# Five half gates of a hybrid decoder layer move from plain tiles into groups with a seven-product scheme

## The chip, the cores and the metric

The kernel runs on one core of one Trainium2 chip. The metric is device time in microseconds (us). Five engines matter: PE (TensorE, matrix products and transposes), ACT (ScalarE), DVE (VectorE), POOL (GpSimd, nearly idle here) and SP (SyncE, which issues the weight loads). Each executes its own instructions in the order of the program and waits for the others by semaphores.

## What is computed

A decoder layer on 256 positions of 2048 channels in float32. One wide projection of the normed input feeds three token mixers (attention, gated linear attention, spatial gating) and three gates. The part that the change touches begins where the mixers have delivered their outputs:

```python
    proj = xn @ w_in
    ...
    qa, ka, va, qb, kb, vb, rb, lrb, uc, vc, ga, gb, gc = jnp.split(proj, splits, axis=-1)
    ...
    merged = (jax.nn.sigmoid(ga) * (y_a @ wa) + jax.nn.sigmoid(gb) * (y_b @ wb)
              + jax.nn.sigmoid(gc) * (y_c @ wc))
    h = x + merged @ w_o
    hn = rms_norm(h, n2)
    return h + jnp.square(jax.nn.relu(hn @ w1)) @ w2
```

`ga`, `gb`, `gc` are the three gates, each 2048 wide, and each needs a product of the whole normed input (2048 deep) with its own 2048 columns of `w_in`.

## The kernel before

**Precision.** Every float32 operand is split in two fp32r parts, high and low: ACT copies the high part (`whi`, `fhi`), DVE subtracts it from the operand and leaves the low part (`wlo`, `flo`). A product of two blocks is then three matmuls: high by high, high by low, low by high. Activations stand transposed in `xT`, `yT`, `mT`, `hT` and `fT`, split once; the weights are split as they stream in, so each megabyte of weights costs ACT and DVE a pass each.

**Plain groups.** `group_a` (L214 on) makes 512 output columns for both halves of the positions: for two k-tiles at a time it splits a weight piece of 128x1024 (L203, L204) and runs twelve matmuls of 128x512 (L221 to L223), six for each half of the positions. After every such piece `step()` may emit one queued job, such as a transpose. Before, the three gates and the three branch products were all made so, 512 columns at a time: a loop of four rounds over `n`, with three gates (sigmoid on ACT, L710) and three branch products (multiplied and added on DVE, L715 and L717) in each. In this stretch the order on the engines is the scheduler's.

**Fixed-order groups.** The output projection (`w_o`) and the feed-forward (`w_ff1`, `w_ff2`) run as `Group` objects of 1024 columns, with the order of all four busy engines written out (`manual_schedule`). A group of 2048 deep consists of eight pairs of k-tiles, taken as its order string says. A pair written `P` is a plain one: 24 matmuls. A pair written `S` uses the seven-product scheme for 2x2 blocks and takes 21: it comes in two pieces, A (9 matmuls) and B (12). For an S pair DVE first forms sums of weight blocks (`fsum`, L807 to L809), and these are split too. The other operand of an S pair are four sums of activation blocks (`sums`, made in `turn_into` on L683 to L689 from a transposed tile `half`, of which there are two buffers): four DVE operations on 128x128 blocks, an ACT copy of the high part (L688), a DVE subtraction for the low part (L689). `hT` and `fT` have three S pairs (3, 5, 6), the merged tile `mT` has two (6, 7).

**Order of work.** The loop over pieces `i` emits the split of piece `i + 2` (`ready`, `LEAD = 2`), then the matmuls of piece `i`. The split parts have three buffers. A group with S pairs ends by combining its eight accumulators on DVE (`seven` and four adds), and its results are transposed into the next activation tile while the next group runs: the transposes of one half (`turns`) stand after that group's first piece, those of the other half in the middle of its second piece.

**What sets the time of a turn.** In `turn_into` the block sums of a tile stand right behind its copies: ACT copies `half` from PSUM, copies the high part, then waits for DVE's four block sums, then copies their high part.

Of the kernel before, what the change touches and what calls it, by code (L numbers as in the profile page):

```python
# [11 lines left out]
F32 = mybir.dt.float32  # L12
# [6 lines left out]
P = 128  # L19
T = 256  # L20
# [43 lines left out]
def trunk(ctx: ExitStack, tc: tile.TileContext, x, rpe_table, norm1_g, w_in, q_norm_g, k_norm_g,  # L64
# [598 lines left out]
    def turn_into(dst, ks, srcs, gain=None, kinds=None, fn=AF.Copy):  # L663

        banks = []
        for s in srcs:
            banks.append(bank("tt"))
            transpose4(banks[-1], s)
        for k, ps in zip(ks, banks):
            if kinds is None:  # L670
                split_ps(dst[:, k:k + 2, :], v3(ps, 2))
                continue
            a = mpool.tile([P, 2, T], F32, tag="half", name="half", bufs=2)
            if gain is None:
# [54 lines left out]
    mg_ctx.__exit__(None, None, None)
    w_ctx.__exit__(None, None, None)  # L730
    ffp = ctx.enter_context(tc.tile_pool(name="ffp", bufs=1, reuse_waits="tile"))
    hT = acts.tile([P, KT, 2 * T], F32R, tag="act0", name="hT")

    sums = acts.tile([P, 8, 2, 4, P], F32R, tag="act1", name="sums")
    hS = {kp: sums[:, i] for i, kp in enumerate(SEVEN)}
    fS = {kp: sums[:, 4 + i] for i, kp in enumerate(SEVEN)}
    mS.update({kp: sums[:, 4 + i] for i, kp in enumerate(SEVEN_O)})
    hsq = gpool.tile([P, NT, 4], F32, name="hsq")
    r2 = gpool.tile([P, NT], F32, name="r2")
    hs = gpool.tile([P, NT], F32, name="hs")  # L740
# [259 lines left out]
```

## Time and profile before

| | us |
|---|---|
| median of 3 runs | 1455.39 |
| lowest, highest | 1454.23, 1455.61 |
| the profiled execution, its own time | 1454.36 |
| its span | 1452.6 |
| gates and branches, about | 303 to 649 |
| `w_o`, feed-forward, about | 649 to 1447 |

The span is what the profile covers; the execution's own time is 1.76 us longer. Times below are counted from the span's start. The granted clock of PE is given as a share of full speed: 1.00 is 2.4 GHz, 0.50 is 1.2 GHz. An engine's idle time counts only where the work that ends last waits in it.

### The profile page before, as it was taken

To read this page: it belongs to the slowest core of one execution; us is meant where nothing else is said; L and a number is where in the kernel's file an instruction comes from. 1 tells how busy PE (TensorE), PEld (TensorE's weight loads), DVE (VectorE), ACT (ScalarE), POOL (GpSimd) and SP (SyncE) were. 2 spreads that over 40 slices of the span, in tenths; PEclk is the share of its full clock that TensorE was granted. 3 is DMA by queue.
4 is the path that set the end of the run, shared out by engine and by line. 5 is a ranking of instruction groups with operands and counts; after the bars stand their busy time and mean duration, and the time that the engine had idled before them with its cause. 6 is when DMAs were issued, how large, how long until landed. Compare 5 with 4: busy or idle time off the path is not lost.

```text
span 1452.6 us, 16287 instructions
## 1 busy us (share of the span) xinstructions
PE 1422.9 (98%) x6452; PEld 1168.5 (80%) x6452; DVE 1072.9 (74%) x1160; ACT 766.5 (53%) x827; POOL 14.0 (1%) x37
## 2 busy tenths in 40 slices
PE   8999999999999999999998999999999999999998
PEld 6899887788888888877886878888788887888776
DVE  5655655454645546457898989999999999999898
ACT  7457444454444444445656654466644665546653
POOL 2000000000000000000000000000000000000000
PEclk9999999999999999999999999999999999999999
DMA  8555554545555555545555555666456555555553
GB/s 290 183 181 165 182 176 133 184 151 199 192 185 203 177 199 187 190 158 193 199 185 192 173 175 197 208 203 203 147 200 207 199 203 174 201 190 194 198 195 124
DMA packets 101948, 272.20 MB, mean 187 GB/s; under 512 B 4748, under 2 KB 11440, under 8 KB 101872
## 3 DMA queue, kind: packets, MB, share of 16 engines
q1 hardware_dynamic: 100944, 268.59, 55.0%
q0 software_dynamic: 928, 2.57, 0.5%
q8 instruction: 50, 0.82, 0.2%
q14 instruction: 26, 0.21, 0.0%
HBM read 268.26 MB, written 2.88 MB: 187 GB/s over the span
## 4 chain that ended last, share of the span: by engine, by line
PE 70%; DVE 18%; issue 6%; ACT 5%; DMA 0%; SPq 0%; DVEq 0%; ACTq 0%
PE c L768 22%; PE ga L221 14%; PE ga L223 14%; PE ga L222 14%; DVE flo L795 8%; PE P L768 4%; DVE fsum L807 3%; ACT fhi L794 3%; DVE fsum L808 2%; DVE fsum L809 2%; PE tt L235 1%; DVE fT L175 1%; PE pst L590 0%; ACT sums L688 0%; ACT half L675 0%
## 5 line engine op out<-in xcount | busy, mean ns | idle before, releaser
L204 DVE TENSOR_TENSOR wlo<-wraw,whi 128x1024 fp32r<-128x1024 f32 (+3 forms) x232 | 266.2, 1152 | 248.6 <-ACT whi L203 248.4
L203 ACT ACTIVATE whi<-wraw 128x1024 fp32r<-128x1024 f32 (+3 forms) x232 | 231.4, 1002 | 292.4 <-PE ga L223 284.9
L794 ACT ACTIVATE fhi<-fraw 128x2048 fp32r<-128x2048 f32 (+2 forms) x145 | 252.9, 1750 | 163.6 <-PE c L768 115.3
L795 DVE TENSOR_TENSOR flo<-fraw,fhi 128x2048 fp32r<-128x2048 f32 (+2 forms) x145 | 300.0, 2080 | 48.0 <-ACT fhi L794 48.0
L221 PE MATMUL ga<-whi,xT 128*128 128x512 f32 (+2 forms) x768 | 297.8, 388 | 0.0
L222 PE MATMUL ga<-wlo,xT 128*128 128x512 f32 (+2 forms) x768 | 293.4, 382 | 0.0
L223 PE MATMUL ga<-whi,xT 128*128 128x512 f32 (+2 forms) x768 | 293.1, 382 | 0.0
L768 PE MATMUL c<-fhi,hT 128*128 128x512 f32 x736 | 237.7, 390 | 0.0
L768 PE MATMUL c<-fhi,fT 128*128 128x512 f32 x736 | 237.1, 390 | 0.0
L221 PEld LDWEIGHTS ga<-whi,xT 128*128 128x128 f32 x768 | 144.6, 188 | 29.8 <-issue 3.9
L223 PEld LDWEIGHTS ga<-whi,xT 128*128 128x128 f32 x768 | 144.6, 188 | 26.9
L222 PEld LDWEIGHTS ga<-wlo,xT 128*128 128x128 f32 x768 | 144.7, 188 | 25.0
L768 PEld LDWEIGHTS c<-fhi,hT 128*128 128x128 f32 x736 | 138.2, 188 | 28.6
L768 PEld LDWEIGHTS c<-fhi,fT 128*128 128x128 f32 x736 | 138.2, 188 | 28.4
L794 ACT ACTIVATE fhi<-fsum 128x1024 fp32r<-128x1024 f32 x104 | 108.6, 1059 | 85.7 <-DVE fsum L807 41.0
L768 PE MATMUL c<-flo,fT 128*128 128x512 f32 x368 | 143.7, 391 | 3.3 <-DVE flo L795 3.3
L768 PE MATMUL c<-flo,hT 128*128 128x512 f32 x368 | 143.2, 389 | 0.0
L795 DVE TENSOR_TENSOR flo<-fsum,fhi 128x1024 fp32r<-128x1024 f32 x104 | 122.5, 1219 | 1.4 <-ACT fhi L794 1.4
L768 PE MATMUL P<-fhi,sums 128*128 128x512 f32 x312 | 106.0, 394 | 4.2 <-ACT fhi L794 4.0
L768 PEld LDWEIGHTS c<-flo,fT 128*128 128x128 f32 x368 | 69.1, 188 | 19.1 <-DVE flo L795 4.9
L768 PEld LDWEIGHTS c<-flo,hT 128*128 128x128 f32 x368 | 69.1, 188 | 14.1
L768 PEld LDWEIGHTS P<-fhi,sums 128*128 128x128 f32 x312 | 59.3, 190 | 18.4 <-ACT fhi L794 6.3
(260 smaller groups left out, 1427.1 us busy)
## 6 DMA issues: line engine op xcount, KB each, us to landing
fraw<-in_w_ff_dram SPq DMA_DIRECT2D x128, 1024.0 KB, 5.0
wraw<-in_w_in_dram SPq DMA_DIRECT2D x80, 1024.0 KB, 4.9
fraw<-in_w_o_dram SPq DMA_DIRECT2D x16, 1024.0 KB, 5.3
wraw<-in_w_br_b_dram SPq DMA_DIRECT2D x8, 1024.0 KB, 5.0
wraw<-in_w_in_dram SPq DMA_DIRECT2D x8, 692.0 KB, 4.1
wraw<-in_w_br_a_dram SPq DMA_DIRECT2D x4, 1024.0 KB, 4.9
wraw<-in_w_br_c_dram SPq DMA_DIRECT2D x4, 1024.0 KB, 5.4
wraw<-in_w_in_dram SPq DMA_DIRECT2D x6, 512.0 KB, 11.4
```

Of the source, the lines that this page charges most:

```text
L175: nc.vector.tensor_tensor(lo, ps, hi.bitcast(F32), ALU.subtract)
L203: nc.scalar.activation(hi[:, j:j + per, :w], src, AF.Copy)
L204: nc.vector.tensor_tensor(lo[:, j:j + per, :w], src, hi[:, j:j + per, :w].bitcast(F32), ALU.subtract)
L221: mm(ps[tt][:, :w], xh, hi[:, j, :w], start=(k == 0), stop=False)
L222: mm(ps[tt][:, :w], xh, lo[:, j, :w], start=False, stop=False)
L223: mm(ps[tt][:, :w], xl, hi[:, j, :w], start=False, stop=(k == nk - 1))
L768: mm(self.banks[role], a, w, start=(n == 0), stop=(n == self.total[role] - 1))
L794: nc.scalar.activation(hi[:, i:e], src[:, i - a:e - a], AF.Copy)
L795: nc.vector.tensor_tensor(lo[:, i:e], src[:, i - a:e - a], hi[:, i:e].bitcast(F32), ALU.subtract)
L807: nc.vector.tensor_tensor(ts[:, 0:2], raw[:, 1:3], raw[:, 0:1].to_broadcast([P, 2, GW]), ALU.add)
L808: nc.vector.tensor_add(ts[:, 2], ts[:, 0], raw[:, 2])
L809: nc.vector.tensor_add(ts[:, 3], ts[:, 2], raw[:, 3])
```

## The change

- The first half (1024 columns) of the first gate stays plain, in two `group_a` of 512 columns; the second of them now lies inside the written-out order. The other five half gates become groups of 1024 columns with the order `ORDER_G`, four S pairs (2, 3, 5, 6) and four P pairs. The branch products become groups of P pairs alone, 1024 columns wide, with two, four and two pairs.
- The S pairs of the gates need block sums of the normed input. `xs_turn` makes them for four pairs: four transposes of `h`, two scaling copies on ACT, then the block sums at once. The four calls stand behind the first four pieces of the second `group_a`.
- `w_o` has its S pairs at 2 and 3 instead of 6 and 7, in another order.
- `turn_into` no longer makes the block sums on the spot: they are emitted one piece later, behind the split that `ready` emits there (`run(i, "early")`). The squares for the second norm now stand behind the split of one piece more.
- From the first gate on there is one pool layout: the merged tile takes `yT`'s place, `hT` takes `xT`'s, `fT` takes the merged tile's; the block sums share two small pools; there are three `fu` buffers.

```diff
-ORDER_O = "P0 P1 P2 P3 P4 S6 S7 P5".split()
-SEVEN = [int(c[1]) for c in ORDER if c[0] == "S"]
-SEVEN_O = [int(c[1]) for c in ORDER_O if c[0] == "S"]
+ORDER_O = "P0 P1 S2 P6 S3 P4 P5 P7".split()
+ORDER_G = "P0 P1 S2 S3 P4 S5 S6 P7".split()
...
+    pg = [group_a(w_in[0], 0, KT, C_GATE, 512, xT)]
+    drain()
+    br_ctx.__exit__(None, None, None)
+    early_ctx.__exit__(None, None, None)
...
+    def kinds_of(pairs, tag, bufs, per):
+        out = {}
+        for i in range(0, len(pairs), per):
+            t = ffp.tile([P, per, 2, 4, P], F32R, tag=tag, name="kinds", bufs=bufs)
...
+        nc.scalar.activation(s[:, 0], b, AF.Copy)
+        nc.vector.tensor_tensor(s[:, 1], b, s[:, 0].bitcast(F32), ALU.subtract)
...
-            a = mpool.tile([P, 2, T], F32, tag="half", name="half", bufs=2)
+            a = ffp.tile([P, 2, T], F32, tag="half", name="half", bufs=2)
...
             if k // 2 in kinds:
-
-                b = a.rearrange("p j (t c) -> p (j t) c", c=P)
-                nc.vector.tensor_sub(b[:, 3], b[:, 1], b[:, 3])
-                nc.vector.tensor_sub(b[:, 1], b[:, 0], b[:, 1])
-                nc.vector.tensor_sub(b[:, 0], b[:, 3], b[:, 0])
-                nc.vector.tensor_add(b[:, 2], b[:, 2], b[:, 0])
-                s = kinds[k // 2]
-                nc.scalar.activation(s[:, 0], b, AF.Copy)
-                nc.vector.tensor_tensor(s[:, 1], b, s[:, 0].bitcast(F32), ALU.subtract)
...
+                rest.append(lambda a=a, s=kinds[k // 2]: block_sums(a, s))
+
+        def sums():
+            for f in rest:
+                f()
+        return sums if rest else None
...
-            pg = group_a(w_in[0], 0, KT, C_GATE + i * D + n * 512, 512, xT)
...
-            pp = group_a(wsrc[0], 0, nk, n * 512, 512, yT, k0=k0)
-            for tt in range(NT):
-                nc.vector.tensor_mul(gts[i][tt], pp[tt], gts[i][tt])
-                if i:
-                    nc.vector.tensor_add(gts[0][tt], gts[0][tt], gts[i][tt])
...
-            return [lambda: None, lambda: turns(hT, n, 1, src, V_N2, hS, AF.Copy),
-                    lambda: turns(hT, n, 0, src, V_N2, hS, AF.Copy), norm]
+            return [None, lambda: turns(made["hT"], n, 1, src, n2c, hS, AF.Copy),
+                    lambda: turns(made["hT"], n, 0, src, n2c, hS, AF.Copy), norm]
...
+            def sigmoid():
+                for tt in range(NT):
+                    v = u[:, 2 * tt:2 * tt + 2]
+                    nc.scalar.activation(v, v, AF.Sigmoid, scale=r[:, tt:tt + 1])
+            if (i, hf) == (2, 1):
+                mS.update(kinds_of(seven_of(ORDER_O), "xs", 1, 4))
+                m = gates[0, 0]
+                return [sigmoid, lambda: merged_turn(0, 0, m), lambda: merged_turn(0, 1, m)]
+            return [sigmoid]
...
+                    nc.vector.tensor_mul(v, g.banks[f"c{tt + 1}{2 - c}"], v)
+            if i:
+                m = gates[0, hf]
+                nc.vector.tensor_add(m, m, u)
+            if (i, hf) == (2, 1):
+                hS.update(kinds_of(seven_of(ORDER), "fu", 3, 2))
+                made["hT"] = acts.tile([P, KT, 2 * T], F32R, tag="act0", name="hT")
+                return [None, lambda: merged_turn(1, 1, m), lambda: merged_turn(1, 0, m)]
...
+    mT = yT
+    made = {}
+    xS = kinds_of(seven_of(ORDER_G), "xs", 1, 4)
...
+    for hf in range(2):
+        for i, (wsrc, k0, nk) in enumerate(((w_br_a, 0, 4), (w_br_b, 4, 8), (w_br_c, 12, 4))):
+            if (i, hf) != (0, 0):
+                groups.append(Group(w_in[0], 0, C_GATE + i * D + hf * W2, xT, xS, ORDER_G, *gate_in(i, hf)))
+            groups.append(Group(wsrc[0], 0, hf * W2, yT, {}, [f"P{j}" for j in range(nk // 2)], *branch_in(i, hf), k0))
...
+    def xs_turn(kp):
+        srcs = [h[:, tt, (2 * kp + j) * P:(2 * kp + j + 1) * P] for j in range(2) for tt in range(NT)]
+        turn_into(None, [2 * kp], [srcs], g1[0], xS)()
+
+    todo = {}
+
+    def run(i, when):
+        for fn in todo.pop((i, when), ()):
+            rest = fn and fn()
+            if rest:
+                todo.setdefault((i + 1, "early"), []).insert(0, rest)
+
+    fetched = []
     with tc.manual_schedule(engines=ORDERED):
+        u = gates[0, 0] = new_u()
+
+        def first_sigmoid(c):
+            for tt in range(NT):
+                nc.scalar.activation(u[:, 2 * tt + c], pg[c][tt], AF.Sigmoid, scale=r[:, tt:tt + 1])
+        first_sigmoid(0)
+        for kp in seven_of(ORDER_G):
+            later(lambda kp=kp: xs_turn(kp))
+        pg.append(group_a(w_in[0], 0, KT, C_GATE + 512, 512, xT))
+        w_ctx.__exit__(None, None, None)
+        hlp = ctx.enter_context(tc.tile_pool(name="hlp", bufs=1, side="right", reuse_waits="tile"))
         for i in range(LEAD):
             ready(i)
+        first_sigmoid(1)
...
-            since = i - done
-            if since == 1 and after:
-                after[0]()
-            multiply(piece, wts.pop(i), half=after[2] if since == 2 and after else None)
-            if since == 1 and after:
-                after[1]()
-            if since == 2 and len(after) > 3:
-                after[3]()
-            step()
+            run(i, "early")
+            multiply(piece, wts.pop(i), half=lambda: run(i, "half"))
+            run(i, "half")
+            run(i, "late")
             if ends:
-                after, done = g.last(g), i
+
+                for (d, when), fn in zip(((1, "early"), (1, "late"), (2, "half"), (3, "early")), g.last(g)):
+                    todo.setdefault((i + d, when), []).append(fn)
 
 
 # ---- launch: one core; inputs and outputs as the reference has them ----
```

ACT's instructions around the first gate's end, before (names: `whi` a weight piece's high part, `yT` the branch input, `ga` an accumulator of a gate, `gt` the gate, numbers tell tiles apart):

```order
L203 ACTIVATE whi<-wraw 128x1024 x2
L174 ACTIVATE yT<-ybt 128x2x256
L203 ACTIVATE whi<-wraw 128x1024 x3
L710 ACTIVATE gt_2587<-ga_2412,r 128x512
L710 ACTIVATE gt_2587<-ga_2413,r 128x512
L203 ACTIVATE whi<-wraw 128x1024 x8
```

The same place now (`half` is a transposed tile, `kinds` the block sums, `fu` the gate):

```order
L208 ACTIVATE whi<-wraw 128x1024 x2
L179 ACTIVATE yT<-ybt 128x2x256
L208 ACTIVATE whi<-wraw 128x1024
L1015 ACTIVATE fu<-ga_2412,r 128x512
L1015 ACTIVATE fu<-ga_2413,r 128x512
L208 ACTIVATE whi<-wraw 128x1024
L707 ACTIVATE half<-tt,g_150 128x256 x2
L692 ACTIVATE kinds<-half 128x512
L208 ACTIVATE whi<-wraw 128x1024
L707 ACTIVATE half<-tt,g_150 128x256 x2
L692 ACTIVATE kinds<-half 128x512
L208 ACTIVATE whi<-wraw 128x1024
```

Before, two or more splits of the next group stood ahead of the sigmoids; now the sigmoids stand ahead of the next group's first split, and two `half` copies and one `kinds` copy stand ahead of each of the four splits after it.

ACT in the first `w_ff2` group of a phase, from the first turn on, before:

```order
L688 ACTIVATE sums<-half 128x512
L675 ACTIVATE half<-tt 128x512
L174 ACTIVATE fT<-half 128x2x256
L794 ACTIVATE fhi<-fraw 128x1536
L675 ACTIVATE half<-tt 128x512
L174 ACTIVATE fT<-half 128x2x256
L675 ACTIVATE half<-tt 128x512
L174 ACTIVATE fT<-half 128x2x256
L688 ACTIVATE sums<-half 128x512
L794 ACTIVATE fhi<-fsum 128x1024 x2
L794 ACTIVATE fhi<-fraw 128x2048
```

The same place now:

```order
L772 ACTIVATE fhi<-fraw 128x1536
L692 ACTIVATE kinds<-half 128x512
L704 ACTIVATE half<-tt 128x512
L179 ACTIVATE fT<-half 128x2x256
L704 ACTIVATE half<-tt 128x512
L179 ACTIVATE fT<-half 128x2x256
L772 ACTIVATE fhi<-fsum 128x1024 x2
L692 ACTIVATE kinds<-half 128x512
L772 ACTIVATE fhi<-fraw 128x2048
```

Each copy of block sums moved behind a split: the first from ahead of the A piece (`fhi<-fraw` 128x1536) to behind it, the second from ahead of the B piece (`fhi<-fsum`) to between it and the next P piece (`fhi<-fraw` 128x2048).

## Rows read from the trace of the kernel before

**Rows 1.** The page, parts 1 and 4: busy engines, and the last chain by engine.

```profile
PE 1422.9 (98%) x6452; PEld 1168.5 (80%) x6452; DVE 1072.9 (74%) x1160; ACT 766.5 (53%) x827; POOL 14.0 (1%) x37
...
PE 70%; DVE 18%; issue 6%; ACT 5%; DMA 0%; SPq 0%; DVEq 0%; ACTq 0%
```

**Rows 2.** Stretches: span, busy PE, PEld, DVE, ACT, POOL, granted clock, DMA share, GB/s.

```profile
313.00:648.00 335.00, 335.00 (x1491) 277.35 (x1490) 173.03 (x164) 149.18 (x153) 0.00 (x0) 1.00 0.57 189
649.20:651.80 2.60, 0.19 (x1) 0.00 (x0) 2.56 (x5) 0.00 (x0) 0.00 (x0) 1.00 0.23 16
652.10:655.40 3.30, 3.30 (x9) 2.52 (x9) 2.99 (x2) 0.00 (x0) 0.00 (x0) 0.50 0.94 344
...
762.60:768.10 5.50, 0.92 (x3) 0.19 (x1) 2.29 (x5) 5.41 (x12) 0.00 (x0) 1.00 0.31 124
768.20:771.40 3.20, 3.12 (x7) 2.48 (x8) 2.81 (x3) 2.89 (x2) 0.00 (x0) 0.50 0.00 0
...
1027.00:1048.50 21.50, 19.51 (x83) 14.93 (x82) 19.85 (x22) 13.37 (x11) 0.00 (x0) 1.00 0.45 152
```

**Rows 3.** Timeline of PE: start, us, instruction, count; in brackets idle time before.

```profile
316.30 0.39 PE L221 MATMUL ga<-whi,xT 128*128 128x512 f32 x1
...
335.34 0.39 PE L221 MATMUL ga<-whi,xT 128*128 128x512 f32 x1
...
651.81 0.61 PE L768 MATMUL c<-flo,mT 128*128 128x512 f32 x1 [2.42 <-DVE flo L795]
...
748.12 1.03 PE L235 MATMUL tt<-ident,h 128*128 128x128 f32 x8
...
767.02 0.50 PE L768 MATMUL P<-fhi,sums 128*128 128x512 f32 x1 [4.00 <-ACT fhi L794]
768.28 0.80 PE L768 MATMUL P<-flo,sums 128*128 128x512 f32 x1 [0.76 <-DVE flo L795]
...
1032.21 0.50 PE L768 MATMUL P<-flo,sums 128*128 128x512 f32 x1 [0.76 <-DVE flo L795]
...
1046.93 0.50 PE L768 MATMUL P<-flo,fT 128*128 128x512 f32 x1 [0.37 <-DVE flo L795]
```

**Rows 4.** Groups of instructions, 290 to 660: busy, mean ns, idle time before.

```profile
L204 DVE TENSOR_TENSOR wlo<-wraw,whi 128x1024 fp32r<-128x1024 f32 x128 | 156.8, 1225 | 167.6 <-ACT whi L203 167.6
...
L203 ACT ACTIVATE whi<-wraw 128x1024 fp32r<-128x1024 f32 x128 | 135.7, 1060 | 180.8 <-PE ga L223 179.3 <-issue 1.5
...
L710 ACT ACTIVATE gt<-ga,r 128x512 f32<-128x512 f32 x22 | 15.2, 690 | 10.7 <-PE ga L223 10.7
```

**Rows 5.** The same for 850 to 1360, the feed-forward.

```profile
L795 DVE TENSOR_TENSOR flo<-fraw,fhi 128x2048 fp32r<-128x2048 f32 x59 | 133.9, 2287 | 28.4 <-ACT fhi L794 28.4
...
L794 ACT ACTIVATE fhi<-fraw 128x2048 fp32r<-128x2048 f32 x59 | 113.1, 1917 | 63.8 <-PE c L768 31.5 <-issue 20.6 <-DMA fraw<-in_w_ff_dram 11.5
...
L795 DVE TENSOR_TENSOR flo<-fsum,fhi 128x1024 fp32r<-128x1024 f32 x72 | 84.8, 1219 | 0.8 <-ACT fhi L794 0.8
...
L794 ACT ACTIVATE fhi<-fsum 128x1024 fp32r<-128x1024 f32 x72 | 75.1, 1059 | 62.1 <-PE c L768 28.9 <-DVE fsum L807 26.8 <-DVE fsum L809 6.4
...
L795 DVE TENSOR_TENSOR flo<-fraw,fhi 128x1536 fp32r<-128x1536 f32 x36 | 63.0, 1751 | 0.0
...
L807 DVE TENSOR_TENSOR fsum<-fraw 128x1024 f32<-128x1024 f32 x35 | 42.8, 1222 | 0.4
...
L808 DVE TENSOR_TENSOR fsum<-fsum,fraw 128x512 f32<-128x512 f32 x36 | 24.9, 692 | 1.2
```

**Rows 6.** Timeline of ACT and DVE in turns of `hT` and `fT`.

```profile
748.76 0.84 ACT L678 ACTIVATE half<-tt,cols 128x256 f32<-128x256 f32 x2 [3.96 <-PE tt L235]
...
1018.70 0.29 DVE L683 TENSOR_TENSOR half<-half 128x128 f32<-128x128 f32 x1
...
1019.68 0.29 DVE L686 TENSOR_TENSOR half<-half 128x128 f32<-128x128 f32 x1
...
1020.00 0.63 ACT L688 ACTIVATE sums<-half 128x512 fp32r<-128x512 f32 x1 [2.06 <-DVE half L686]
```

More of the change, by code (lines that the diff above doesn't have):

```diff
@@ L729, in trunk @@
[L729 to L738, printed above, removed]
@@ L739, in trunk, with __init__ @@
-    r2 = gpool.tile([P, NT], F32, name="r2")
-    hs = gpool.tile([P, NT], F32, name="hs")
+                rest.append(lambda a=a, s=kinds[k // 2]: block_sums(a, s))
[3 more added lines that the diff above has]
+        return sums if rest else None
     W2 = 2 * GW
     class Group:
-        def __init__(self, src, r0, c0, act, sums, order, first, last):
+        def __init__(self, src, r0, c0, act, sums, order, first, last, k0=0):
             self.src, self.r0, self.c0, self.act, self.sums, self.order = src, r0, c0, act, sums, order
+            self.k0 = k0
@@ L895, in last @@
             b, u = g.banks, g.u
+            if not fS:
+                fS.update(kinds_of(seven_of(ORDER), "xs", 1, 4))
+                made["fT"] = acts.tile([P, KT, 2 * T], F32R, tag="act1", name="fT")
             for i, name in ((1, "c11"), (3, "c21"), (0, "c12"), (2, "c22")):
@@ L930, in add_in, with gate_in, first, last @@
         return first, last
-    groups = [Group(w_o[0], 0, n * W2, mT, mS, ORDER_O, *residual(n)) for n in range(2)]
+    def gate_in(i, hf):
+        def first(g):
+            g.u = seven(g)
+        def last(g):
+            b, u = g.banks, g.u
+            gates[i, hf] = u
+            for j, name in ((1, "c11"), (3, "c21"), (0, "c12"), (2, "c22")):
+                nc.vector.tensor_add(u[:, j], u[:, j], b[name])
+            def sigmoid():
[7 more added lines that the diff above has]
+            return [sigmoid]
+        return first, last
@@ new lines, in merged_turn, with src, branch_in, last @@
+    def merged_turn(n, c, m):
+        def src(tt, c0):
+            return m[:, 2 * tt + c0 // GW, c0 % GW:c0 % GW + P]
+        return turns(mT, n, c, src, None, mS, AF.Copy)
+    def branch_in(i, hf):
+        def last(g):
+            u = gates[i, hf]
+            for tt in range(NT):
+                for c in (1, 0):
+                    v = u[:, 2 * tt + c]
+                    nc.vector.tensor_mul(v, g.banks[f"c{tt + 1}{2 - c}"], v)
[6 more added lines that the diff above has]
+                return [None, lambda: merged_turn(1, 1, m), lambda: merged_turn(1, 0, m)]
+            return []
+        return lambda g: None, last
@@ L933, in trunk @@
+    for n in range(2):
+        groups.append(Group(w_o[0], 0, n * W2, mT, mS, ORDER_O, *residual(n)))
     for ph in range(FF // D):
-        fT = mpool.tile([P, KT, 2 * T], F32R, tag="act2", name="fT") if ph == 0 else fT
         for n in range(2):
-            groups.append(Group(w_ff1[0], 0, ph * D + n * W2, hT, hS, ORDER, *square_in(ph, n)))
+            groups.append(Group(w_ff1[0], 0, ph * D + n * W2, "hT", hS, ORDER, *square_in(ph, n)))
         for n in range(2):
-            groups.append(Group(w_ff2[0], ph * D, n * W2, fT, fS, ORDER, *add_in(ph, n)))
+            groups.append(Group(w_ff2[0], ph * D, n * W2, "fT", fS, ORDER, *add_in(ph, n)))
```

83 lines of the change are left out of this document (35 added, 48 removed).

## The prediction

> **What bounds the kernel now.** I read the page first, then the stretches, then PE's own timeline. PE is busy 98% of the span, and the chain that ended last runs 70% through PE and 18% through DVE [rows 1]. In the gates and branches, 313 to 648, PE has no idle microsecond at all, at the full clock, while DVE works 173 of 335 us and ACT 149 [rows 2]: there only the number of matmuls counts, and a split of weights (`whi` 1.06, `wlo` 1.23 us) is long done when PE wants it [rows 4]. From 649 on the timeline of PE shows waits in a few places only [rows 3]: 2.42 us at the entry to `w_o` (651.81, on `flo`), 4.00 and 0.76 at the entry to the feed-forward (767.02 and 768.28, on `fhi` and `flo` of an S pair), and waits of 0.76 and 0.37 in the first `w_ff2` group of a phase, where the stretch 1027 to 1048.5 leaves PE 2.0 of 21.5 us idle [rows 2, 3]. Right after the first two entries the granted clock is 0.50, the 1.2 GHz level, for some 3.3 us (652.1 and 768.2) [rows 2]; PE had been idle most of the 2.6 and 5.5 us before. So the kernel is a dense row of matmuls, and what counts is how many it loses and how many new waits it gets.
>
> **The gain: 60 matmuls.** From 316.30 to 335.34 lie 84 matmuls of 128x512, so one costs 0.2267 us [rows 3]. An S pair takes 21 where a P pair takes 24. Five half gates with four S pairs each: 5 x 4 x 3 = 60 matmuls, 60 x 0.2267 = -13.6 us. `w_o` keeps two S pairs, only elsewhere; the branch products keep their matmuls. The Trainium skill ("TensorE: Matmul & The Clock Gate", section "Back-to-back issue gap") gives two paces for 512 columns, 131 ns sustained and about 216 ns isolated. The trace has 227 ns and decides; by the page the gain would be 7.9 or 13.0 us.
>
> **What PE gets in addition.** `xs_turn` adds 16 transposes. Eight take 1.03 us [rows 3]: +2.0 us.
>
> **The gate groups.** A P pair gives PE 24 x 0.2267 = 5.44 us, an S pair 4.76. DVE needs 2.29 for a P pair (one `flo` of 2048), and for an S pair 1.22 + 2 x 0.69 for the sums, then 1.75 + 2 x 1.22 for the low parts: 6.8 [rows 5]. Two S pairs in a row leave DVE behind by 2 x (6.8 - 4.76) = 4.1 us, two P pairs around them give 2 x (5.44 - 2.29) = 6.3 back. The lead of two pieces holds a few microseconds more, and the feed-forward runs the same kind of pairs with waits under 1 us [rows 3]. I cost the inside of the groups at nothing. What hides it is this slack; if it isn't there, each half gate waits about the 4.1 us, 20 in all.
>
> **The entry and the four `xs_turn`s.** This is the largest term. In the second `group_a` the order is by hand. Its splits have no lead: each is emitted just ahead of its own matmuls, and a turn stands behind them. On ACT the order after the first piece is two `half` copies, one `kinds` copy, and only then the next `whi`. The `kinds` copy needs DVE's four block sums, these need the `half` copies, these need the transposes, and these stand on PE behind all matmuls of the piece before. So from the transposes to the next matmul runs one chain with nothing beside it: two `half` copies 0.84, four sums 1018.70 to 1019.97 = 1.27, `kinds` 0.63 [rows 6], `whi` 1.06 [rows 4], and four hand-overs of about 0.1 (1019.97 to 1020.00 between DVE and ACT; 0.13 from half of the transposes at 748.12 to the copy at 748.76) [rows 3, 6]: 4.2 us. Then PE runs one matmul and waits for `wlo`, 1.23 less 0.23: 1.0 us. That is 5.2 for each turn, and nothing else is queued on PE: 4 x 5.2 = 20.8. At the entry of this group two sigmoids (0.69 each, at the end of the first `group_a`) now stand ahead of the first split: 1.38 + 1.06 + some 0.6 of hand-overs and `wlo` less the first matmul: +3.0. Sum +23.8. Before, the splits stood ahead of the sigmoids, and PE lost nothing here.
>
> **`w_o`.** Before, its two groups waited about 4.2 us together, most of it the 2.42 at the entry and what follows it. Now in the first group the B piece of pair 2 and the split of pair 6 come behind eight turn copies of the merged tile and two `kinds`; walking it with the durations above I get 7.4, so +3.2. In the second group P6's split stands behind the same kind of copies, and I take again +3.2, by likeness. Together +6.4; the bounds are 0 (the lead hides all) and 10.
>
> **The feed-forward.** Here the deferred block sums decide. The move helps the A piece of the S pair (its `fhi` no longer waits for a turn's sums) and burdens the next: P4's `fhi` of 2048 now stands behind the second `kinds`, which waits for DVE's sums, and these stand on DVE behind the three sums and the `flo` of B3. Walked from the group's start at 0: PE does P0 with its turn until 6.5, P1 and its turn until 13.1, P2 until 18.5, A3 until 20.6, B3 until 23.5. DVE ends B3's low parts at 22.1, the block sums at 23.4; ACT copies them until 24.1 and makes P4's high part (1.92 [rows 5]) until 26.0; DVE makes the low part (2.29) until 28.2. PE waits 2.4 and then about 2.0, in place of the 2.0 to 2.5 it loses in this group now, and part of the older waits stays: +1.8. The first group of `w_ff1` is fed in the same manner from the turn of its predecessor: +1.8. Two such groups in each of four phases: 3.6 x 4 = +14.4. The first `w_ff1` group after `w_o` has also the squares of the norm ahead of the split: +1.2. Bounds for both together: -3 (only the A piece's gain is left) and +24 (if the low part's 2.29 is paid in full in each).
>
> **The clock.** Two waits of 2.4 us and more are each followed by a stretch at 0.50 [rows 2, 3]; waits of 0.8 are not. Such a stretch of 3.3 us holds about 1.65 us of work at full clock, so it costs up to 1.7. I count some twelve waits of over 2 us (four `xs_turn`s, two in `w_o`, two at the feed-forward's entry, four in `w_ff2`), against two before: ten more at 1.3, since part of the slow time falls on waits for `wlo` and `flo` anyway: +13.0. Bounds 0 and 17.
>
> **Sum.** -13.6 + 2.0 + 23.8 + 6.4 + 14.4 + 1.2 + 13.0 = +47.2. Against the profiled execution: 1454.36 + 47.2 = 1501.6; the median stands 1.03 above it, so 1502.6, taken as 1503.
>
> **The rivals.** *Faster.* One mechanism: the splits of the coming piece are in front of every block sum, so that PE never sees the chains. For this speaks that the deferred sums stand behind a split in the new order; against it that this split is not the one PE wants next, and that the second `group_a` has no lead. It decides where ACT's next split is ready before PE ends the piece. Then -13.6 + 2.0, 9 us of the entry waits (2.42, 4.00, 0.76 and the slow clock after them) and 3.4 of the `w_ff2` waits go: 1455.4 - 24 = 1431 to 1439, middle 1435. Chance 0.10. *The `xs_turn` chain alone is covered*, by splits made earlier than I read them: 20.8 and four slow stretches of 1.3 less, 1477. Chance 0.10. *The feed-forward stays as it is*, since DVE is further ahead in P2 than I walked: 14.4 and four slow stretches less, 1483. Chance 0.12. *More slow clock*, or DVE bounding the gate groups: the second piece of each chain also runs at 0.50, or part of the 20 us of the gate groups appears: 1513. Chance 0.08.
>
> **How the numbers follow.** The forecast, 1503, has the remaining 0.60. The range for 8 in 10 takes in the two partial rivals with some of their own spread and the slower one: 1465 to 1517. Faster by over 0.2% (2.9 us, about what a measurement of this kernel can tell from no change) is the first rival less its edge: 0.09; within 0.2% that edge and a case in which both partial rivals hold, 0.03; slower 0.88.
>
> **What the changed profile would show.** Right: four waits of PE of about 4.2 us on `whi` and 1.0 on `wlo` between 305 and 350, with ACT's `kinds` waiting for DVE; granted clock 0.50 after them; half gates without a wait, 4 x 5.44 + 4 x 4.76 = 40.8 us each; a wait of some 2 us at P4 of the first `w_ff2` group of each phase and a feed-forward longer by 12 to 20 us; new waits at the second and sixth pair of `w_o`. Wrong: no waits on `whi` near 305 to 350, gate groups with waits on `flo`, or a feed-forward of the same length. My weakest numbers are the walks in the feed-forward and in `w_o`, where one copy earlier or later on ACT turns 2 us into 0.

## The result and the profile after

The changed kernel takes 1500.76 us (median of 4 runs, 1499.5 to 1503.41) beside 1454.91 for the kernel before: a ratio of 1.0317, 95% interval 1.03 to 1.0335. The forecast was 1503, the range 1465 to 1517. The profiled execution has a span of 1498.5 us against 1452.6, so 45.9 us more, of 47.2 forecast.

The page of the changed kernel, parts 1 and 4, to be read beside [rows 1]:

```profile
PE 1431.7 (96%) x6408; PEld 1169.9 (78%) x6408; DVE 1180.8 (79%) x1252; ACT 794.9 (53%) x824; POOL 14.2 (1%) x37
...
PE 40%; DVE 22%; ACT 9%; issue 7%; DVEq 0%; ACTq 0%
```

PE does 44 instructions less and is yet busy 9 us longer: a matmul at granted clock 0.50 stands longer in its busy time (starts 0.43 us apart instead of 0.23, rows below). Its share of the span falls from 98 to 96%. The shares of the chain that ended last are not to be set against each other: before they add up to 99%, after only to 78%, since there the chain could be followed back no further than 327.7 us.

Where the time lies is read from three stretches: the gates and branches from the first matmul of the first gate (after its early start), `w_o`, and the feed-forward with the end. Columns: stretch, its length, busy time of PE, PEld, DVE, ACT and POOL with instructions, granted clock, DMA share, GB/s. Before:

```profile
308.70:649.00 340.30, 340.30 (x1516) 281.73 (x1514) 175.94 (x167) 151.79 (x156) 0.00 (x0) 1.00 0.57 189
649.00:742.70 93.70, 89.85 (x398) 73.14 (x397) 77.03 (x80) 50.48 (x53) 0.00 (x0) 0.98 0.58 197
742.70:1452.60 709.90, 690.25 (x3073) 563.39 (x3071) 644.34 (x643) 397.22 (x368) 0.00 (x0) 1.00 0.55 188
```

After:

```profile
309.40:669.70 360.30, 339.46 (x1463) 276.51 (x1462) 281.28 (x256) 180.70 (x149) 0.00 (x0) 0.97 0.53 184
669.70:771.70 102.00, 93.48 (x405) 74.64 (x404) 81.28 (x86) 51.77 (x57) 0.00 (x0) 0.97 0.48 165
771.70:1498.50 726.80, 696.13 (x3073) 568.51 (x3071) 642.70 (x640) 395.48 (x368) 0.00 (x0) 0.98 0.53 182
...
327.00:367.00 40.00, 22.35 (x62) 16.05 (x63) 14.62 (x26) 11.50 (x19) 0.00 (x0) 0.70 0.27 105
385.70:427.00 41.30, 41.19 (x182) 33.78 (x182) 37.89 (x35) 22.41 (x17) 0.00 (x0) 1.00 0.56 190
```

| stage | before | after | difference | forecast, slow clock included |
|---|---|---|---|---|
| before the first gate | 308.7 | 309.4 | +0.7 | 0 |
| gates and branches | 340.3 | 360.3 | +20.0 | -13.6 + 2.0 + 23.8 + 5.2 = +17.4 |
| `w_o` | 93.7 | 102.0 | +8.3 | 6.4 + 1.3 = +7.7 |
| feed-forward and end | 709.9 | 726.8 | +16.9 | 14.4 + 1.2 + 6.5 = +22.1 |

(The forecast's ten stretches of low clock at 1.3 us are four in the gates, two less one in `w_o`, six less one from there on.) All three stages got longer, although PE executes fewer matmuls in the first. The stretch 327 to 367, in which the four `xs_turn`s lie, leaves PE idle for 17.6 of 40 us at a mean granted clock of 0.70; the half gate at 385.7 to 427 has PE busy 41.19 of 41.3 us.

**The second xs_turn**, all three engines, timeline: start, us, engine, line, instruction, in brackets idle time before and what ended it.

```profile
336.27 0.60 PE L240 MATMUL tt<-ident,h 128*128 128x128 f32 x4
336.90 0.84 ACT L707 ACTIVATE half<-tt,g 128x256 f32<-128x256 f32 x2 [6.17 <-PE tt L240]
...
338.75 0.29 DVE L691 TENSOR_TENSOR half<-half 128x128 f32<-128x128 f32 x1
339.14 0.63 ACT L692 ACTIVATE kinds<-half 128x512 fp32r<-128x512 f32 x1 [1.40 <-DVE half L691]
339.68 1.04 ACT L208 ACTIVATE whi<-wraw 128x1024 fp32r<-128x1024 f32 x1
...
340.75 1.23 DVE L209 TENSOR_TENSOR wlo<-wraw,whi 128x1024 fp32r<-128x1024 f32 x1 [0.25 <-ACT whi L208]
340.77 0.80 PE L226 MATMUL ga<-whi,xT 128*128 128x512 f32 x1 [3.90 <-ACT whi L208]
342.03 0.80 PE L227 MATMUL ga<-wlo,xT 128*128 128x512 f32 x1 [0.47 <-DVE wlo L209]
...
343.05 0.63 PE L226 MATMUL ga<-whi,xT 128*128 128x512 f32 x1
343.48 0.63 PE L227 MATMUL ga<-wlo,xT 128*128 128x512 f32 x1
```

It is the chain of the forecast: transposes, two `half` copies (0.84), four sums (the last at 338.75), `kinds` (0.63), `whi` (1.04), first matmul 3.90 us after PE went idle; then `wlo`, and PE waits again. ACT is idle 6.17 us ahead of the copies and could have made this `whi` there (in e1_lead, below, it does), but in its order `kinds` comes first, and `kinds` waits for DVE. The Trainium skill says the same of the queues ("PSUM — Partial Sum Buffer", section "Engine vs sequencer instructions": ACT's and DVE's are strict FIFO); the rows agree, `whi` (339.68) stands behind `kinds` (339.14). Behind the wait the matmuls start 0.43 us apart (343.05, 343.48), the granted clock is 0.50 there. The Trainium skill gives N / 1.2 for that level ("TensorE: Matmul & The Clock Gate", section "Back-to-back issue gap"), an estimate of 427 ns for 512 columns, and the trace agrees; its full-speed figures differ from the 227 ns of [rows 3], and there the rows decide.

**P4 of the first `w_ff2` group of the third phase:**

```profile
1247.02 0.29 DVE L691 TENSOR_TENSOR half<-half 128x128 f32<-128x128 f32 x1
1247.35 0.63 ACT L692 ACTIVATE kinds<-half 128x512 fp32r<-128x512 f32 x1 [2.66 <-DVE half L691]
1247.88 3.27 ACT L772 ACTIVATE fhi<-fraw 128x2048 fp32r<-128x2048 f32 x2
...
1249.81 2.29 DVE L773 TENSOR_TENSOR flo<-fraw,fhi 128x2048 fp32r<-128x2048 f32 x1 [1.11 <-ACT fhi L772]
1249.83 0.50 PE L746 MATMUL c<-fhi,fT 128*128 128x512 f32 x1 [1.63 <-ACT fhi L772]
...
1252.16 0.50 PE L746 MATMUL c<-flo,fT 128*128 128x512 f32 x1 [1.83 <-DVE flo L773]
```

`kinds` waits 2.66 us for the last of DVE's sums; P4's high part comes behind it, its low part behind that, and PE waits 1.63 and 1.83 us. The wait of 0.76 us at the B piece of this group's first S pair before [rows 3] is gone: the deferral does what it says there, and pays more for it at P4.

### The profile page after: what moved, and what is told of

It reads as the page before. It is cut to its first block, busy times and chain, and to the rows that moved or that the text cites. A ratio compares the mean times of both kernels' runs of the same rounds, so it can differ in the third digit from the quotient of the medians.

```text
span 1498.5 us, 16263 instructions
## 1 busy us (share of the span) xinstructions
PE 1431.7 (96%) x6408; PEld 1169.9 (78%) x6408; DVE 1180.8 (79%) x1252; ACT 794.9 (53%) x824; POOL 14.2 (1%) x37
## 4 chain that ended last, share of the span: by engine, by line
PE 40%; DVE 22%; ACT 9%; issue 7%; DVEq 0%; ACTq 0%
PE c L746 32%; DVE flo L773 11%; PE P L746 5%; ACT fhi L772 5%; DVE fsum L785 4%; DVE fsum L786 2%; DVE fsum L787 2%; ACT half L704 1%; ACT fT L179 1%; PE ga L227 1%; ACT half L707 1%; PE ga L228 1%; PE ga L226 0%; ACT kinds L692 0%; ACT fu L885 0%
## 5 line engine op out<-in xcount | busy, mean ns | idle before, releaser
L773 DVE TENSOR_TENSOR flo<-fraw,fhi 128x2048 fp32r<-128x2048 f32 (+2 forms) x201 | 417.1, 2084 | 91.4 <-ACT fhi L772 87.8
L772 ACT ACTIVATE fhi<-fraw 128x2048 fp32r<-128x2048 f32 (+2 forms) x201 | 351.3, 1754 | 255.2 <-PE c L746 192.8
L209 DVE TENSOR_TENSOR wlo<-wraw,whi 128x1024 fp32r<-128x1024 f32 (+3 forms) x120 | 128.8, 1083 | 100.9 <-ACT whi L208 100.7
L226 PE MATMUL ga<-whi,xT 128*128 128x512 f32 (+2 forms) x448 | 176.4, 395 | 17.4 <-ACT whi L208 17.4
L208 ACT ACTIVATE whi<-wraw 128x1024 fp32r<-128x1024 f32 (+3 forms) x120 | 112.4, 946 | 124.8 <-PE ga L228 116.9
L227 PE MATMUL ga<-wlo,xT 128*128 128x512 f32 (+2 forms) x448 | 172.6, 385 | 2.9 <-DVE wlo L209 2.9
L228 PE MATMUL ga<-whi,xT 128*128 128x512 f32 (+2 forms) x448 | 171.5, 383 | 0.0
L746 PE MATMUL c<-fhi,yT 128*128 128x512 f32 x464 | 149.2, 395 | 1.6 <-ACT fhi L772 1.6
L746 PE MATMUL P<-fhi,kinds 128*128 128x512 f32 x432 | 145.3, 390 | 0.5 <-ACT fhi L772 0.4
L746 PE MATMUL c<-fhi,xT 128*128 128x512 f32 x400 | 130.5, 389 | 0.0
L226 PEld LDWEIGHTS ga<-whi,xT 128*128 128x128 f32 x448 | 86.6, 193 | 36.9 <-ACT whi L208 18.8
L746 PEld LDWEIGHTS c<-fhi,yT 128*128 128x128 f32 x464 | 88.5, 191 | 20.8 <-ACT fhi L772 2.5
L228 PEld LDWEIGHTS ga<-whi,xT 128*128 128x128 f32 x448 | 86.2, 192 | 14.6
```

What stands on the lines that cost most here:

```text
L208: nc.scalar.activation(hi[:, j:j + per, :w], src, AF.Copy)
L209: nc.vector.tensor_tensor(lo[:, j:j + per, :w], src, hi[:, j:j + per, :w].bitcast(F32), ALU.subtract)
L226: mm(ps[tt][:, :w], xh, hi[:, j, :w], start=(k == 0), stop=False)
L227: mm(ps[tt][:, :w], xh, lo[:, j, :w], start=False, stop=False)
L228: mm(ps[tt][:, :w], xl, hi[:, j, :w], start=False, stop=(k == nk - 1))
L746: mm(self.banks[role], a, w, start=(n == 0), stop=(n == self.total[role] - 1))
```

## The experiments

**Theory:** the time is lost where ACT's copy of block sums waits for DVE ahead of a split that PE needs: in the four `xs_turn`s, in `w_o`, in the feed-forward, with the low clock on top. **Rivals:** the new pool layout (tiles that share buffers), too much work for DVE in the S pairs of the gates, or the S pairs' place in `w_o`.

### The second group_a with a lead (e1_lead)

```diff
+    def group_lead(src, r0, nk, c0, w, act, then):
+        ps = [bank(f"ga{tt}") for tt in range(NT)]
+        it = weights(src, r0, nk, c0, w)
+        made = [next(it), next(it)]
+        then()
+        for q in range(nk // KQ):
+            made += [x for x in [next(it, None)] if x]
+            products(ps, act, 0, q, nk, *made.pop(0), w)
+            step()
+        return ps
...
-        pg.append(group_a(w_in[0], 0, KT, C_GATE + 512, 512, xT))
+        pg.append(group_lead(w_in[0], 0, KT, C_GATE + 512, 512, xT, lambda: None))
```

> The second group_a gets the lead of two pieces that the fixed-order groups have: its splits are emitted two pieces ahead of their matmuls, the four xs_turns and all else stay. Theory (the chain of half copies, four sums, kinds, whi and wlo stands alone on the path, because the group has no lead): the four waits of 4.0 and 1.0 us on whi and wlo vanish, 20 us, and the stretches of granted clock 0.50 between 332 and 366, some 35 matmuls at 0.43 instead of 0.23 us, 7 us more: 1473 to 1476. Rival (block sums of the normed input are too much work for ACT and DVE wherever they stand; ACT needs 0.84 + 1.27 + 0.63 + 1.06 = 3.8 us per piece against PE's 3.2): the waits shrink to 1 us or so each but remain, 1482 to 1488. Rival (the turns are not what costs): 1500.

Measured: 1476.43 us (1476.19 to 1476.83), 24.3 less than the changed kernel. The gates' stage, and PE at the first turn:

```profile
309.80:646.50 336.70, 332.11 (x1463) 272.02 (x1462) 280.89 (x256) 180.25 (x149) 0.00 (x0) 0.99 0.58 197
...
327.00:351.00 24.00, 22.42 (x103) 17.48 (x103) 15.47 (x27) 14.49 (x21) 0.00 (x0) 1.00 0.45 174
```

```profile
328.09 0.60 PE L252 MATMUL tt<-ident,h 128*128 128x128 f32 x4
328.45 0.48 PE L226 MATMUL ga<-whi,xT 128*128 128x512 f32 x1
...
342.15 0.50 PE L227 MATMUL ga<-wlo,xT 128*128 128x512 f32 x1 [0.76 <-DVE wlo L209]
...
346.26 0.50 PE L227 MATMUL ga<-wlo,xT 128*128 128x512 f32 x1 [0.76 <-DVE wlo L209]
```

The stage shrinks from 360.3 to 336.7 us, PE runs on 0.36 us after a turn's first transpose, and the clock is 1.00 from 327.2 to 351. Two waits of 0.76 us on `wlo` are left, where ACT has fallen behind (it takes 3.8 to 4.1 us from turn to turn, as the rival had it, but the lead holds most of it), and the waits at the group's entry are now followed by a slow stretch, 323.8 to 327.2; so the time is 0.4 us above what was expected. The missing lead cost 24 us, about half of the 46.

### The chain's idle time filled (e11_fill)

```diff
         turn_into(None, [2 * kp], [srcs], g1[0], xS)()
+        j = bank("fill")
+        for n in range(16):
+            mm(j, xT[:, n, 0:P], xT[:, n, :], start=(n == 0), stop=(n == 15))
```

> Behind the four transposes of each xs_turn PE gets 16 matmuls of 128x512 whose result nobody reads, 16 x 0.2267 = 3.6 us, just under the 4.0 us in which it waits for whi there; all else as changed. It measures the clock's share by itself. Theory (the stretches at 0.50 follow from PE's idleness, and 33 matmuls at 0.43 instead of 0.23 us cost some 6.7 us): PE stays at 1.00 between 330 and 366, the next piece starts at the same place, and the time falls by 5 to 7 us to 1494 to 1496 though PE does 64 matmuls more. Rival (the slow stretches cost nothing, since the chain of splits sets the pace anyway, or the fill delays the chain): 1500 or more.

Measured: 1492.51 us (1491.93 to 1494.22), 8.3 less than the changed kernel and a little more than expected; in the profile the gates' stage is 6.9 us shorter.

```profile
309.00:662.40 353.40, 346.37 (x1526) 282.54 (x1525) 281.28 (x256) 180.73 (x149) 0.00 (x0) 1.00 0.55 188
...
327.00:367.00 40.00, 35.99 (x156) 27.51 (x155) 18.13 (x29) 16.32 (x22) 0.00 (x0) 1.00 0.31 116
```

```profile
334.56 3.92 PE L1002 MATMUL fill<-xT 128*128 128x512 f32 x16
...
338.72 0.50 PE L226 MATMUL ga<-whi,xT 128*128 128x512 f32 x1 [0.23 <-ACT whi L208]
339.98 0.50 PE L227 MATMUL ga<-wlo,xT 128*128 128x512 f32 x1 [0.76 <-DVE wlo L209]
```

Sixty-four matmuls more, and the kernel is faster: the chain still ends 4 us after the transposes, but the granted clock stays at 1.00 in the same 40 us where it was 0.70. So of e1_lead's 24 us some 7 were the clock's, and some 17 the waits themselves.

### Block sums on the spot again (e2_spot)

```diff
-                rest.append(lambda a=a, s=kinds[k // 2]: block_sums(a, s))
+                block_sums(a, kinds[k // 2])
...
-        turn_into(None, [2 * kp], [srcs], g1[0], xS)()
+        turn_into(None, [2 * kp], [srcs], g1[0], xS)
```

> turn_into makes the block sums on the spot again, as in the kernel before; orders, layout and xs_turns stay as changed. Theory (the deferral puts P4's high part behind the kinds copy that waits for DVE's sums): the feed-forward goes back from 177.4 to 173.8 us per phase and loses its waits at P4, about 16 to 17 us in all: 1482 to 1487, with w_o changed by 3 us or less. Rival (the feed-forward is slower because of the new pool layout, the block sums and fu tiles sharing buffers): the phase stays at 177.4, 1498 to 1502.

Measured: 1481.24 us (1480.53 to 1482.45), 19.5 less, just below the 1482 that was expected at least. The feed-forward:

```profile
771.20:1480.20 709.00, 689.55 (x3073) 562.46 (x3071) 641.44 (x640) 396.77 (x368) 0.00 (x0) 1.00 0.55 187
```

It takes 709.0 us, within 1 us of the kernel before (709.9), and a phase takes 173.9 us again. The new layout and the shared buffers are still in this kernel, so they cost the feed-forward nothing that shows; the deferral of the sums costs it all of its 17 us. `w_o` takes 100.0 us here, 2 us less than in the changed kernel.

### Only the copy deferred (e4_hybrid)

```diff
         nc.vector.tensor_add(b[:, 2], b[:, 2], b[:, 0])
+        return lambda: split_sums(b, s)
+
+    def split_sums(b, s):
         nc.scalar.activation(s[:, 0], b, AF.Copy)
...
-                rest.append(lambda a=a, s=kinds[k // 2]: block_sums(a, s))
+                rest.append(block_sums(a, kinds[k // 2]))
```

> Only half of the block sums is deferred: DVE's four sums stand on the spot, ACT's kinds copy and DVE's subtraction one piece later behind the split. Theory (P4 waits because ACT's kinds copy waits for DVE sums that stand behind the sums and low parts of the B piece): ACT no longer waits for DVE at the kinds copy, P4's wait falls from 2.0 and 2.3 us to about 1.5 in all, and the low-clock stretches in the feed-forward go: 1484 to 1490. Rival (P4 waits for its low part because DVE as a whole has too much work in that stretch): the waits stay within 0.5 us of what they are, 1496 to 1501.

Measured: 1471.69 us (1469.56 to 1476.98), 29.1 less, about twice what was expected; 27.2 of it in the feed-forward. The feed-forward, and ACT and DVE ahead of P4 in the third phase:

```profile
769.80:1469.40 699.60, 686.46 (x3073) 562.67 (x3071) 640.56 (x640) 396.85 (x368) 0.00 (x0) 1.00 0.56 190
```

```profile
1222.99 0.29 DVE L691 TENSOR_TENSOR half<-half 128x128 f32<-128x128 f32 x1
1223.20 2.35 DVE L776 TENSOR_TENSOR flo<-fsum,fhi 128x1024 fp32r<-128x1024 f32 x2
1223.31 0.64 ACT L695 ACTIVATE kinds<-half 128x512 fp32r<-128x512 f32 x1 [0.17 <-DVE half L691]
1223.85 3.28 ACT L775 ACTIVATE fhi<-fraw 128x2048 fp32r<-128x2048 f32 x2
...
1226.07 2.28 DVE L776 TENSOR_TENSOR flo<-fraw,fhi 128x2048 fp32r<-128x2048 f32 x1
```

`kinds` waits 0.17 instead of 2.66 us, P4's high and low parts follow without a gap, and PE has no wait there. The expectation left 1.5 us at P4 and forgot the entry of the feed-forward, where the waits of 4.58 and 1.53 us become 1.05 and 1.83 and the stretch at 0.50 is gone (the first two `w_ff1` groups take 91.3 instead of 97.6 us). The rival, that DVE has too much work there, falls: the same DVE work, issued earlier, fits. With 699.6 us this feed-forward is 10 us shorter than that of the kernel before, 8.3 of it in the `w_ff2` groups and 2.8 at the entry. It keeps the deferral's good side (the 0.76 us of [rows 3] at 1032.21 are gone here too) without the bad one.

### The old order in `w_o` (e3_order_o)

```diff
-ORDER_O = "P0 P1 S2 P6 S3 P4 P5 P7".split()
+ORDER_O = "P0 P1 P2 P3 P4 S6 S7 P5".split()
```

> w_o takes its pairs in the old order, S pairs 6 and 7 near the end; all else as changed. Theory (the early S pair 2 and P6 stand right behind the turn copies and sums): w_o goes from 104 back to about 94 us and the half-speed stretch at 742 goes: 1489 to 1492. Rival (it is the deferred sums, not the place of the S pairs, that delay the splits in w_o): the waits move to the pairs behind the new place of the sums and the time stays at 1497 to 1502.

Measured: 1489.12 us (1488.28 to 1489.93), 11.6 less.

```profile
671.40:760.40 89.00, 88.38 (x405) 72.94 (x404) 77.93 (x83) 52.06 (x57) 0.00 (x0) 1.00 0.54 184
```

`w_o` takes 89.0 us against 102.0 in the changed kernel and 93.7 before (the other parts of the profiled execution are 2.5 us longer than there, so that 10.5 are left of the 13.0). With the early S pairs ACT stands ahead of the splits with two `kinds` copies that wait for DVE; in the changed kernel:

```profile
681.06 0.63 ACT L692 ACTIVATE kinds<-half 128x512 fp32r<-128x512 f32 x1 [9.65 <-DVE half L691]
...
683.63 0.63 ACT L692 ACTIVATE kinds<-half 128x512 fp32r<-128x512 f32 x1 [1.94 <-DVE half L691]
...
684.80 0.50 PE L746 MATMUL P<-fhi,yT 128*128 128x512 f32 x1 [1.70 <-ACT half L704]
...
686.46 1.99 ACT L772 ACTIVATE fhi<-fsum 128x1024 fp32r<-128x1024 f32 x2
...
687.56 0.50 PE L746 MATMUL P<-fhi,kinds 128*128 128x512 f32 x1 [0.41 <-ACT fhi L772]
```

The B piece's high part (686.46) is behind both `kinds` and four copies of the second half's turn, much as the forecast had it; PE waits at 684.80 (released, by the profile, by a `half` copy) and 687.56, and on until 694.93. The rival falls: the deferral is still in e3_order_o, and its `w_o` has no such waits, while e2_spot has the new order without the deferral, and its `w_o` takes 100.0 us.

### Fewer S pairs in the gates (e5_dose)

```diff
-ORDER_G = "P0 P1 S2 S3 P4 S5 S6 P7".split()
+ORDER_G = "P0 P1 S2 S3 P4 P5 P6 P7".split()
+XS = [2, 3, 5, 6]
...
-    xS = kinds_of(seven_of(ORDER_G), "xs", 1, 4)
+    xS = kinds_of(XS, "xs", 1, 4)
...
-        for kp in seven_of(ORDER_G):
+        for kp in XS:
```

> The five half gates keep two S pairs (2, 3) and take pairs 5 and 6 as plain ones; the four xs_turns stay, the block sums of pairs 5 and 6 are made and not used. All else as changed. Theory (an S pair saves three matmuls and the groups are dense): 5 x 2 x 3 = 30 matmuls more, 30 x 0.2267 = +6.8: 1507 to 1508. Rival (what the S pairs save in matmuls is lost again, since DVE needs 6.8 us for each against PE's 4.76): 1499 to 1502.

Measured: 1506.6 us (1505.49 to 1508.1), 5.8 more than the changed kernel, just below what was expected. The gates' stage grows by 5.1 us (365.4); a half gate takes 42.16 instead of 41.20 us. 42.16 is 186 x 0.2267, a dense row; the half gate with four S pairs, 180 matmuls, would be 40.8 when dense and is 0.4 longer. Of the 6.8 us that were counted 4.8 show in the five half gates. The rival falls: the saving is real, and the larger part of the count.

### All mends together, and what the S pairs are then worth (e7_all, e9_spread, e10_plain)

e7_all has e1_lead's lead with the first gate's sigmoids behind the first two splits, e4_hybrid's split of the sums and the old `ORDER_O`:

```diff
-        first_sigmoid(0)
...
-        pg.append(group_a(w_in[0], 0, KT, C_GATE + 512, 512, xT))
+        pg.append(group_lead(w_in[0], 0, KT, C_GATE + 512, 512, xT, lambda: first_sigmoid(0)))
```

> Three mends together: the second group_a with a lead of two pieces, its first two splits also ahead of the first gate's sigmoids; DVE's sums on the spot with the kinds copy deferred; w_o in the old order. If their gains add (24 from the lead, 4 to 5 from the entry of that group, 29 from the half deferral, 7 to 9 from w_o, which the half deferral has partly mended): 1434 to 1440, faster than the kernel before by 15 to 20 us. Rival (they share waits and slow-clock stretches, so that one gain is counted twice): 1445 to 1455.

Measured: 1435.12 us (1432.41 to 1435.9), ratio to the kernel before 0.9861 (0.9846 to 0.9875). The gains add, and the rival falls; stage by stage they differ.

```profile
309.40:641.50 332.10, 330.02 (x1463) 270.77 (x1461) 281.08 (x256) 180.48 (x149) 0.00 (x0) 1.00 0.59 200
641.50:730.00 88.50, 88.17 (x406) 73.06 (x405) 78.02 (x83) 51.93 (x57) 0.00 (x0) 1.00 0.54 183
730.00:1432.50 702.50, 689.24 (x3073) 564.53 (x3071) 643.07 (x643) 396.72 (x368) 0.00 (x0) 0.99 0.56 190
```

Against the changed kernel `w_o` gains 13.5 us, more than the 7 to 9 expected; the feed-forward gains 24.3, less than the 27.2 of e4_hybrid. Here a stretch at 0.50 of 6.8 us follows the waits at its entry (1.38 and 1.82 us), in e4_hybrid none follows waits of 1.05 and 1.83.

e9_spread puts a free piece between the turns:

```diff
             later(lambda kp=kp: xs_turn(kp))
+            later()
```

> The same with the four xs_turns behind every second piece instead of every piece. Theory (with the lead alone ACT needs 3.9 us per piece with a turn against PE's 3.2, which leaves two waits of 1.0 us at the end of the four turns; with a piece in between it catches up): 2 us less than with the turns in a row, 1432 to 1438. Rival (the later turns delay the first S pairs of the next group): no gain, or 1 to 3 us more.

Measured: 1433.53 us (1431.54 to 1435.19), ratio 0.9852 (0.9838 to 0.9867), the fastest of all. But the theory isn't borne out: the gates' stage takes 332.1 us, as there.

```profile
337.17 0.50 PE L227 MATMUL ga<-wlo,xT 128*128 128x512 f32 x1 [0.77 <-DVE wlo L209]
...
341.29 0.50 PE L227 MATMUL ga<-wlo,xT 128*128 128x512 f32 x1 [0.75 <-DVE wlo L209]
```

```profile
345.18 0.49 PE L761 MATMUL c<-fhi,yT 128*128 128x512 f32 x1 [1.13 <-ACT fhi L787]
346.44 0.50 PE L761 MATMUL c<-flo,yT 128*128 128x512 f32 x1 [0.77 <-DVE flo L788]
```

The two waits of e7_all (first fence) are gone, and two come instead at the first piece of the next group (second fence), as the rival said. The 1.6 us between the medians are no more than the runs scatter (their ranges overlap), and by the profile 1.4 us of them lie in the feed-forward, 0.9 at its entry, which the edit doesn't touch.

e10_plain takes e7_all and makes the five half gates of P pairs alone, without `xs_turn`s:

```diff
-ORDER_G = "P0 P1 S2 S3 P4 S5 S6 P7".split()
+ORDER_G = "P0 P1 P2 P3 P4 P5 P6 P7".split()
...
         def first(g):
-            g.u = seven(g)
+            pass
...
-            b, u = g.banks, g.u
-            gates[i, hf] = u
-            for j, name in ((1, "c11"), (3, "c21"), (0, "c12"), (2, "c22")):
-                nc.vector.tensor_add(u[:, j], u[:, j], b[name])
+            u = gates[i, hf] = new_u()
...
-                    v = u[:, 2 * tt:2 * tt + 2]
-                    nc.scalar.activation(v, v, AF.Sigmoid, scale=r[:, tt:tt + 1])
+                    for c in (1, 0):
+                        nc.scalar.activation(u[:, 2 * tt + c], g.banks[f"c{tt + 1}{2 - c}"], AF.Sigmoid, scale=r[:, tt:tt + 1])
```

> The mended kernel with turns in a row, but the five half gates as fixed-order groups of P pairs alone: no S pairs, no block sums of the normed input, no xs_turns. It tells what the S pairs of the gates are worth when nothing waits for their making. By the count: 60 matmuls more, 13.6, less 2.1 for 16 transposes and 2 to 4 for the waits that the turns still leave: 7 to 11 us slower than with the S pairs. Rival (S pairs in these groups gain nothing): within 2 us of it.

Measured: 1439.98 us (1438.2 to 1441.83), ratio 0.9897 (0.9883 to 0.9912): 4.9 us more than e7_all by the medians, 7.6 by the spans of the profiled executions (1440.1 and 1432.5). The gates' stage:

```profile
310.10:649.30 339.20, 339.20 (x1508) 281.04 (x1506) 166.29 (x96) 140.72 (x102) 0.00 (x0) 1.00 0.58 196
```

339.2 against 332.1: 7.1 us, at the lower end of what was expected; the medians' 4.9 lie below it. The rival (nothing) falls by both. Of the 13.6 us, 2.1 go for transposes, 2.0 for the two waits on `wlo` (each 1.03 from start to start), 1.9 for the five half gates' 0.4 us, which leaves 7.6. So the idea of the change is worth 5 to 7 us where its parts are well placed. Most of what e7_all gains on the kernel before lies elsewhere (`w_o` 88.5 for 93.7 us, feed-forward 702.5 for 709.9): e10_plain, without any S pair in the gates, has 15 of the 20 us too.

## Why the prediction was right, point by point

- **Matmuls, -13.6.** Right in kind, a little large: a half gate of four S pairs takes 41.20 us against 43.52 as P pairs (e10_plain), 2.32 less, 11.6 for five. The 0.4 us each come from a wait on `flo` at the second of two S pairs in a row (S6, at 416.85 in the first half gate); the cost "at nothing" inside the groups was 1.9 us.
- **Transposes, +2.0.** The number is right, the place half: of the sixteen, eight show in the gates' stage (24 before, 32 now) and eight in `w_o` (the same counts), since eight transposes of the merged tile moved there.
- **The `xs_turn`s, +20.8, and the entry, +3.0.** Each turn gave waits of 3.9 and 0.8 us as the profile counts them (0.5 for the second where the matmul ahead of it ran at half clock), 4.2 and 1.3 from start to start of the instructions around them, 0.45 of which are these themselves: 5.0. The entry has waits of 1.72 and 0.76 us at 322.32 and 323.58, some 2.9 in the same count. 22.9 instead of 23.8.
- **The clock in the gates, 4 x 1.3.** Mis-sized: 27 matmuls at 0.43 instead of 0.23 us and a few at the edges, 7.2 us by their starts, and 6.9 by e11_fill, instead of 5.2. The forecast took 0.4 off each 1.7 for slow time that falls into waits. But the stretches after the last three turns lasted 6.8 us, not the 3.4 of before: they began inside the wait (338.9 at the second turn) and still covered 3.7 to 3.9 us of work behind it.
- **`w_o`, +6.4 and 1.3.** The first group's waits add up to some 7 us (7.4 forecast), the second's to some 3 (3.2 forecast, by likeness and not by a walk); there the clock was 0.50 from 741.7 to 748.5. Together +8.3 for 7.7, some 0.9 of it the eight transposes. e3_order_o shows the order as the cause.
- **The feed-forward, +14.4.** The place and the chain were right, the first wait smaller than walked (1.63 and 1.83 at P4, forecast 2.4 and 2.0). Too large was the share of the `w_ff1` groups: such a pair of groups takes 86.6 instead of 85.5 us, +1.1 for 1.8. A pair of `w_ff2` groups without a slow stretch is 1.6 us longer (1.8 forecast). e2_spot and e4_hybrid show the deferral as the cause.
- **The entry of the feed-forward, +1.2 and 1.3.** The first pair of `w_ff1` groups takes 97.6 for 94.1 us, +3.5; with the 1.8 of every such pair 4.3 were forecast. P4's high part stands there behind the deferred `kinds` and the squares of the norm, and PE waits:

```profile
798.00 3.27 ACT L772 ACTIVATE fhi<-fraw 128x2048 fp32r<-128x2048 f32 x2
...
799.95 0.80 PE L746 MATMUL c<-fhi,hT 128*128 128x512 f32 x1 [4.58 <-ACT fhi L772]
```

- **The clock there.** Three of the four phases show a stretch at 0.50 behind P4, the fourth none after the very same waits; 3.8 us in all instead of 5.2. The forecast counted only waits of over 2 us, and these are shorter: here a stretch at 0.50 came also with two waits of 1.63 and 1.83 us that have one matmul between them. In all seven stretches came in addition, not ten, but longer ones; with 7.2 us in the gates, 1.3 in `w_o`, about 1 at the entry and 3.8 here the sum of 13.0 came out about right.
- **The rivals.** "Faster" fell at the point that it named: ACT's next split was not ready. "The feed-forward stays as it is" fell by P4's wait. The two partial ones came true only where a run changed the order for them (e1_lead, e2_spot). Of the slower one (1513) 1.9 us came in the gate groups and some 2 by more slow clock in the gates.

In all the terms missed by +2.6 in the gates, +0.6 in `w_o`, -5.2 in the feed-forward and +0.7 ahead of them, which leaves 45.9 for 47.2. That the total is off by only 1.3 us is partly luck: the misses have both signs, and one alone is 5.2. What made the forecast hold was the order of the instructions on ACT, read beside durations that the trace of before already had.

## What to carry to other kernels

In an order written by hand, a copy that waits for another engine must not stand ahead of a split that the busiest engine needs next: issue the other engine's part early, where it has slack, and the copy late (29 us here). Work put into a loop without a lead costs its whole latency, however little there is of it. And count the clock: a wait of 4 us cost another 1.7 afterwards in the gates here.

## What the runs showed of the hardware

- Matmuls whose result nobody reads paid for themselves: 64 of them in otherwise idle time kept the granted clock at 1.00, and the kernel was faster by 8 us in the medians and 6 in the profiled spans.
- The stretches at half speed differ after like waits: 3.4 us behind the first `xs_turn` (332.1 to 335.5), 6.8 at each of the others, from inside the wait on; in the feed-forward 6.8, 3.4, 3.4 us and none behind four like waits at P4; 6.8 us in e7_all and 3.4 in e9_spread behind the same waits of 1.38 and 1.82 at its entry. What decides between them wasn't tried, and stays open.
